# A hybrid encoder layer on one core: first token tiles split straight from PSUM, first block in halves of 256 columns, loads reordered

## The chip, the cores and the metric

The kernel runs on one core of a Trainium2 chip. The metric is the device time of one execution in microseconds (us). Before the change the median of three runs is 2690.09 us (2688.48 to 2690.36). The engines are TensorE (PE in the profile, its weight loads PEld), VectorE (DVE), ScalarE (ACT), GpSimd (POOL) and SyncE (SP), which issues nearly all of the DMA transfers.

## The reference

One layer on 2048 tokens of width 1024 in float32: a mixing step (windowed attention beside a gated linear recurrence), cross-attention into 256 memory tokens, and a SwiGLU feed-forward, each between RMS norms. The change touches only the beginning:

```python
def rms_norm(x, g):
    y = x * lax.rsqrt(jnp.mean(x * x, axis=-1, keepdims=True) + RMS_EPS)
    return y * g

u = rms_norm(h, g_mix_pre[l])      # 2048 x 1024
z = u @ w_in[l]                    # 1024 x 2816
qa, ka, va, qh, fh, ih, gh = jnp.split(z, IN_SPLITS, axis=-1)
```

## The kernel before, in words

**Products.** A float32 product is made of three float32r products: each operand is split into a part `hi` (rounded to float32r) and a rest `lo = x - hi`, and `hi*hi + hi*lo + lo*hi` is summed in PSUM (L915, L916, L917 in `products`). The weights are the stationary operand (tiles `S`), the tokens the moving one (tiles `T`; the first four are called `u`), 128x512 a matmul. Four 2x2 blocks make a group. Groups of kind "s" use a Strassen-like scheme of seven products (`seven`), kind "p" uses plain eight (`eight`). Of the eleven pairs of weight columns in `ORDER`, the first two are kind "p".

**Token tiles of the input projection.** `in_first` makes the operands of the first 1024 tokens. Half s=0 is tokens 0 to 511, half s=1 tokens 512 to 1023; each has four tiles of 128 tokens. q=0 and q=1 are the two halves of the model width. The four operands are called by step: `T[1]` (q=0, s=0), `T[2]` (q=1, s=0), `T[8]` (q=0, s=1), `T[3]` (q=1, s=1). A plain group runs its steps in the order 1, 2, 8, 3, and each step is 24 matmuls: two output blocks of 12.

For each token tile, `norm` does this: ACT squares the tile and sums it (L397, followed by a read of the accumulator), POOL makes the reciprocal root in two small instructions (L95, L97), DVE scales the tile (L399), PE transposes it in eight 128x128 pieces into two PSUM banks (L430), ACT copies each bank to `raw` in SBUF (L432, 128x512), POOL writes `hi` from `raw` (L837), and DVE writes `lo = raw - hi` (L838). `raw` is needed again later: `resident` makes the operands of the steps 5, 6, 7 and 4 from it (L852 to L861).

The weights of a group come in two loads of two DMAs each (`load` in `in_block`; tile `sraw`), and `streamed` splits them into four `S` tiles, on POOL or ACT (L837, L835) and DVE (L838). There are five `S` buffers and three `sraw` buffers. PSUM has six banks of tag `m` (asked for as "g" or "t") and two of tag `s` (asked for as "s" or "h").

**What sets the order.** The code emits instructions in its own order; that is a priority. When the program is built, a list scheduler with a timing model orders the instructions of each engine by that priority and by when it expects their inputs. On the chip each engine takes its instructions strictly in that fixed order, and SP issues its DMAs in order. `phases` is a generator, advanced by `next`: it first asks for the weights of the first group, then for their `S` tiles, then runs all groups.

Before the change `in_first` issues the loads x0, gain, x1, x2, x3, the four weight DMAs of the first group, x4 to x7 (x0 to x7 are the eight token tiles); it emits `norm(0)` (tiles 0 to 3), the first group's `S` tiles, `mix_consts` (small constants of the mixing step), `norm(1)` (tiles 4 to 7), and then the groups.

## Time and profile before

| what | value |
|---|---|
| median of 3 runs | 2690.09 us |
| the profiled execution | 2685.91 us, of which the span from first to last instruction is 2683.9 us |
| mean granted TensorE clock over the span | 0.985 |
| PE busy | 2588.4 us, 96% of the span |
| DVE, ACT, POOL busy | 1691.2, 1236.3, 500.3 us |
| matmuls | 12362 |
| HBM traffic | 168 GB/s over the span |

The page of the profile gives busy time by engine, then the span in 40 slices of 67 us, then the chain of work that ended last, then groups of instructions. "x<-y" is output and inputs; "128x512" is partitions by elements; "idle before" is the time in which the engine waited just ahead of them, with what released it. The views by time (the timeline, the table of windows, the list of waits) answer for a stretch of the span, in us from its start.

### The profile page before, as it was taken

The page shows a single profiled execution, that of the slowest core. Times are in us where ns is not written, and L with a number is a line of the kernel's source. Part 1 is how long each engine was busy: PE and PEld are TensorE (multiplying, and loading weights), DVE is VectorE, ACT ScalarE, POOL GpSimd, SP SyncE. Part 2 cuts the span into 40 slices and gives each one's busy share as a digit, 9 for nine tenths or more (in the row PEclk, how much of TensorE's full clock was granted, in tenths as well). Part 3 has the DMA queues.
Part 4 walks back from the last instruction along what each step waited for, and adds up shares of the span by engine and source line. Part 5 has one row for each costly group of instructions (what it writes and reads, how often), then busy time and mean ns, then how long its engine had stood idle before and what let it go on. Part 6 is the DMA issues. An engine that isn't in the chain of part 4 may idle for free.

```text
span 2683.9 us, 34591 instructions
## 1 busy us (share of the span) xinstructions
PE 2588.4 (96%) x12362; PEld 2162.3 (81%) x12362; DVE 1691.2 (63%) x2643; ACT 1236.3 (46%) x2581; POOL 500.3 (19%) x683
## 2 busy tenths in 40 slices
PE   6989999999988998999989999999999999999998
PEld 5878788887987887888878888888888888888786
DVE  7675578877544657677666555566555556574666
ACT  4453366655423565555554333343333334443443
POOL 5240344321431332223320000000000000000022
PEclk8999999999999999999999999999999999999999
DMA  5434655455877797376793222262222235586988
GB/s 172 138 123 163 185 158 167 127 147 157 241 231 217 200 259 250 103 237 185 215 299 122 76 82 87 87 225 97 95 82 76 85 127 190 192 249 174 290 214 217
DMA packets 394412, 452.25 MB, mean 169 GB/s; under 512 B 19072, under 2 KB 309888, under 8 KB 394240
## 3 DMA queue, kind: packets, MB, share of 16 engines
q1 hardware_dynamic: 383584, 411.25, 47.4%
q0 software_dynamic: 10656, 38.80, 8.2%
q8 instruction: 97, 1.59, 0.3%
q14 instruction: 75, 0.61, 0.1%
HBM read 315.77 MB, written 134.22 MB: 168 GB/s over the span
## 4 chain that ended last, share of the span: by engine, by line
PE 79%; DMA 9%; DVE 3%; POOL 3%; issue 3%; ACT 2%; SPq 1%; POOLq 0%; DVEq 0%; ACTq 0%
PE psm L917 21%; PE psm L915 21%; PE psm L916 21%; PE psg L153 2%; PE psg L151 2%; PE psg L152 2%; DMA row<-in_w_down_dram 1%; PE pss L1101 1%; DMA row<-h_d 1%; DMA row<-in_w_out_dram 1%; DMA row<-in_x_dram 1%; DMA z<-in_w_out_dram 1%; DMA row<-u_d 1%; DVE S L838 0%; DMA h1t_d<-row 0%
## 5 line engine op out<-in xcount | busy, mean ns | idle before, releaser
L915 PE MATMUL psm<-T,S 128*128 128x512 f32 x2726 | 1060.1, 392 | 24.1 <-ACT part L930 12.6
L916 PE MATMUL psm<-T,S 128*128 128x512 f32 x2726 | 1065.1, 391 | 0.5 <-DVE T L838 0.5
L917 PE MATMUL psm<-T,S 128*128 128x512 f32 x2726 | 1056.6, 391 | 1.7 <-DVE S L838 1.7
L915 PEld LDWEIGHTS psm<-T,S 128*128 128x128 f32 x2726 | 514.4, 189 | 134.6 <-ACT part L930 15.1
L917 PEld LDWEIGHTS psm<-T,S 128*128 128x128 f32 x2726 | 513.8, 188 | 109.9 <-DVE S L838 3.5
L916 PEld LDWEIGHTS psm<-T,S 128*128 128x128 f32 x2726 | 514.3, 189 | 106.7 <-DVE T L838 1.2
L838 DVE TENSOR_TENSOR S<-sraw,S 128x512 fp32r<-128x512 f32 (+1 forms) x327 | 228.8, 704 | 253.8 <-ACT S L835 234.4
L835 ACT ACTIVATE S<-sum 128x512 fp32r<-128x512 f32 (+1 forms) x288 | 173.1, 620 | 327.7 <-PE psm L917 232.4
L838 DVE TENSOR_TENSOR S<-sum,S 128x512 fp32r<-128x512 f32 (+1 forms) x340 | 229.6, 685 | 62.7 <-ACT S L835 38.9
L930 ACT ACTIVATE part<-psm 128x512 f32<-128x512 f32 x249 | 147.5, 597 | 224.5 <-PE psm L917 209.3
L1193 POOL DMA_DIRECT2D row<-y_d x28 | 25.9, 926 | 1136.8 <-DVE T L838 971.7
L835 ACT ACTIVATE S<-sraw 128x512 fp32r<-128x512 f32 (+1 forms) x274 | 168.6, 616 | 128.8 <-PE psm L917 114.8
L838 DVE TENSOR_TENSOR T<-row,T 128x1024 fp32r<-128x1024 f32 (+1 forms) x134 | 159.0, 1193 | 75.4 <-ACT T L835 74.3
L835 ACT ACTIVATE T<-row 128x1024 fp32r<-128x1024 f32 (+1 forms) x134 | 137.3, 1032 | 130.2 <-DVE row L852 34.5
L151 PE MATMUL psg<-u,whi 128*128 128x512 f32 x352 | 142.0, 403 | 2.9 <-POOL whi L135 1.7
L153 PE MATMUL psg<-u,wlo 128*128 128x512 f32 x352 | 139.9, 398 | 0.9 <-DVE wlo L136 0.9
L152 PE MATMUL psg<-u,whi 128*128 128x512 f32 x352 | 140.1, 398 | 0.0
L1164 ACT ACTIVATE junk<-row 128x512 f32<-128x512 f32 x160 | 99.9, 626 | 60.8 <-DVE row L1186 17.9
L136 DVE TENSOR_TENSOR wlo<-raw,whi 128x1024 fp32r<-128x1024 f32 x46 | 59.6, 1295 | 38.3 <-POOL whi L135 36.5
L1316 DVE TENSOR_TENSOR row<-psm,part 128x512 f32<-128x512 f32 x60 | 39.9, 688 | 68.8 <-PE psm L917 68.8
L915 PE MATMUL psm<-u,S 128*128 128x512 f32 x172 | 68.8, 403 | 11.5 <-POOL u L837 8.5
L1325 DVE TENSOR_TENSOR part<-psm,part 128x512 f32<-128x512 f32 x60 | 39.7, 688 | 63.4 <-PE psm L917 63.4
(327 smaller groups left out, 3609.0 us busy)
## 6 DMA issues: line engine op xcount, KB each, us to landing
row<-in_w_down_dram SPq DMA_DIRECT2D x53, 512.0 KB, 7.1
sraw<-in_w_gate_dram SPq DMA_DIRECT2D x44, 512.0 KB, 3.6
sraw<-in_w_up_dram SPq DMA_DIRECT2D x44, 512.0 KB, 3.6
row<-u_d SPq DMA_DIRECT2D x44, 512.0 KB, 7.2
hid_d<-row SPq DMA_DIRECT2D x44, 512.0 KB, 2.6
h_d<-row SPq DMA_DIRECT2D x32, 512.0 KB, 5.2
y_d<-row SPq DMA_DIRECT2D x32, 512.0 KB, 3.2
sraw<-hid_d SPq DMA_DIRECT2D x32, 512.0 KB, 5.3
```

The source lines that it names most:

```text
L136: (lo_engine or nc.vector).tensor_tensor(lo, raw, f32(hi), ALU.subtract)
L151: nc.tensor.matmul(ps, ah, bh, start=(i == 0), stop=False)
L152: nc.tensor.matmul(ps, ah, bl, start=False, stop=False)
L153: nc.tensor.matmul(ps, al, bh, start=False, stop=(i == n - 1))
L835: self.nc.scalar.activation(hi, raw, AF.Copy)
L838: self.nc.vector.tensor_tensor(lo, raw, f32(hi), ALU.subtract)
L915: nc.tensor.matmul(ps, s[:, 0, k, :], t[:, 0, k, :], start=st, stop=False, **kw)
L916: nc.tensor.matmul(ps, s[:, 0, k, :], t[:, 1, k, :], start=False, stop=False, **kw)
L917: nc.tensor.matmul(ps, s[:, 1, k, :], t[:, 0, k, :], start=False, stop=sp, **kw)
L930: nc.scalar.activation(t, ps, AF.Copy)
L1164: self.nc.scalar.activation(junk, a, AF.Square, scale=float(D) ** -0.5, accum_out=to)
L1316: nc.vector.tensor_tensor(d, a, c, ALU.add)
```

## The change

For s=0, `raw` is no longer on the way to the operands. `first` has ACT write `hi` straight from the PSUM bank into `T` and DVE write `lo` from the bank and `hi`; POOL has no part in it. The copies to `raw` (`copied`) come later. Tiles 1 and 2 are transposed into banks of tag `m` ("gt"), tiles 0 and 3 into tag `s`. Half s=1 is made as before (`later`), with `mix_consts` behind it. The first group gets a kind "q": its four `S` tiles are made at once, behind the tiles 0 and 1, and its steps 1 and 2 are done for the columns 0 to 255 (token tiles 0 and 1) and then for 256 to 511. The loads become x0, gain, x1, the first two weight DMAs, x2, x3, the other two, x4 to x7.

```diff
-        def norm(s):
-            ...
-            for i in range(4):
-                x = stage[s][:, i, :]
-                self.normed(x, junk[:, i, :])
-                ...
-                    nc.scalar.activation(raw[q, s][:, :, o], ps.rearrange("p (j t) -> p j t", j=4), AF.Copy)
-                    self.split2(raw[q, s][:, :, o], t[:, 0, :, o], t[:, 1, :, o], "P")
+        def copied(s, i, banks):
+            for q in range(2):
+                nc.scalar.activation(raw[q, s][:, :, i * P:(i + 1) * P], banks[q], AF.Copy)
...
+        def first(i, kinds):
+
+            banks = flipped(0, i, kinds)
+            for q in range(2):
+                hi, lo = parts(0, i, q)
+                nc.scalar.activation(hi, banks[q], AF.Copy)
+                nc.vector.tensor_tensor(lo, banks[q], f32(hi), ALU.subtract)
+            return banks
+
+        def later(i):
+            banks = flipped(1, i, "sh")
+            copied(1, i, banks)
+            for q in range(2):
+                self.split2(raw[q, 1][:, :, i * P:(i + 1) * P], *parts(1, i, q), "P")
...
         next(phases)
-        x_loads(1)
-        norm(0)
-        for _ in range(2):
-            next(phases)
+        x_loads(1, range(4))
+        b0 = first(0, "sh")
+        b1 = first(1, "gt")
+        next(phases)
+        b2 = first(2, "gt")
+        copied(0, 0, b0)
+        b3 = first(3, "sh")
+        copied(0, 1, b1)
+        copied(0, 2, b2)
+        copied(0, 3, b3)
+        next(phases)
+        for i in range(4):
+            later(i)
         self.mix_consts()
-        norm(1)
...
         def load(t, j):
+            if between and j:
+                between()
...
-    TAKES = {"s": (1,) * 7, "p": (2, 2, 0, 0)}
+    TAKES = {"s": (1,) * 7, "p": (2, 2, 0, 0), "q": (4, 0, 0, 0)}
...
-    def eight(self, S, T, nk, out, addend):
+    def eight(self, S, T, nk, out, addend, halves=False):
         a11, a21 = S[:2]
         x, y = self.bank("g"), self.bank("t")
-        self.products(x, [(a11, T[1], nk)], True, False)
-        self.products(y, [(a21, T[1], nk)], True, False)
...
+        if halves:
+
+            a12, a22 = S[2:4]
+            del S[:4]
+            for c in range(2):
+                sl = slice(c * 256, (c + 1) * 256)
+                t1, t2 = T[1][:, :, :, sl], T[2][:, :, :, sl]
+                for ps, a, b in ((x, a11, a12), (y, a21, a22)):
+                    self.products(ps[:, sl], [(a, t1, nk), (b, t2, nk)], True, True)
+                if c:
+                    out(0, 0, x, None)
+                    out(1, 0, y, None)
+                yield
```

`flipped` is the norm and the eight transposes of a tile; `parts` gives the `hi` and `lo` slices of an operand for a tile; `between` is `lambda: x_loads(0, (2, 3))` for the first group and nothing for the others.

More of the change, by code (lines that the diff above doesn't have):

```diff
@@ L404, in in_first, with x_loads @@
         stage = []
-        def x_loads(s):
-            t = self.tb.tile([P, 4, D], F32, tag="T", name=f"x0_{s}", bufs=3)
-            for i in range(4):
-                self.load(t[:, i, :], I["x"][(4 * s + i) * P:(4 * s + i + 1) * P, :])
+        def x_loads(s, tiles):
+            if tiles[0] == 0:
+                stage.append(self.tb.tile([P, 4, D], F32, tag="T", name=f"x0_{s}", bufs=3))
+            for i in tiles:
+                self.load(stage[s][:, i, :], I["x"][(4 * s + i) * P:(4 * s + i + 1) * P, :])
                 if s + i == 0:
                     self.g_mix = self.gain(I["g_mix_pre"])
-            stage.append(t)
-        x_loads(0)
+        x_loads(0, (0, 1))
         junk = self.tb.tile([P, 4, D], F32, tag="T", name="x0_j", bufs=3)
@@ L416, in in_first, with flipped, parts @@
         key = {(0, 0): 1, (1, 0): 2, (0, 1): 8, (1, 1): 3}
-        def norm(s):
+        def flipped(s, i, kinds):
+            x = stage[s][:, i, :]
+            self.normed(x, junk[:, i, :])
+            banks = []
+            for q in range(2):
+                ps = self.bank(kinds[q])
+                for j in range(4):
+                    k = 4 * q + j
+                    nc.tensor.transpose(ps[:, j * P:(j + 1) * P], x[:, k * P:(k + 1) * P], self.ident)
+                banks.append(ps.rearrange("p (j t) -> p j t", j=4))
+            return banks
+        def copied(s, i, banks):
+            for q in range(2):
+                nc.scalar.activation(raw[q, s][:, :, i * P:(i + 1) * P], banks[q], AF.Copy)
+        def parts(s, i, q):
+            o = slice(i * P, (i + 1) * P)
+            return T[key[q, s]][:, 0, :, o], T[key[q, s]][:, 1, :, o]
+        def first(i, kinds):
[4 more added lines that the diff above has]
+                nc.vector.tensor_tensor(lo, banks[q], f32(hi), ALU.subtract)
+            return banks
+        def later(i):
+            banks = flipped(1, i, "sh")
+            copied(1, i, banks)
+            for q in range(2):
+                self.split2(raw[q, 1][:, :, i * P:(i + 1) * P], *parts(1, i, q), "P")
+        for s in range(2):
             for q in range(2):
@@ L421, in norm @@
                 raw[q, s] = self.pair_tile().rearrange("p a d -> p (a d)").rearrange("p (k t) -> p k t", k=4)
-            for i in range(4):
-                x = stage[s][:, i, :]
-                self.normed(x, junk[:, i, :])
-                o = slice(i * P, (i + 1) * P)
-                for q in range(2):
-                    ps = self.bank("sh"[q])
-                    for j in range(4):
-                        k = 4 * q + j
-                        nc.tensor.transpose(ps[:, j * P:(j + 1) * P], x[:, k * P:(k + 1) * P], self.ident)
-                    t = T[key[q, s]]
-                    nc.scalar.activation(raw[q, s][:, :, o], ps.rearrange("p (j t) -> p j t", j=4), AF.Copy)
-                    self.split2(raw[q, s][:, :, o], t[:, 0, :, o], t[:, 1, :, o], "P")
         for q in range(2):
@@ L449, in in_first @@
         get = fetch()
-        blocks = [("p" if i < 2 else "s",) + self.in_block(*p, beside[i], get if i > 9 else ())
+        blocks = [("q" if i == 0 else "p" if i < 2 else "s",)
+                  + self.in_block(*p, beside[i], get if i > 9 else (), None if i else lambda: x_loads(0, (2, 3)))
                   for i, p in enumerate(self.ORDER)]
@@ L474, in in_first, with in_block @@
         return u
-    def in_block(self, ca, cb, beside, get):
+    def in_block(self, ca, cb, beside, get, between):
         nc, w = self.nc, self.I["w_in"]
@@ L821, in swa @@
             yield
-    STEPS = {"s": (1, 5, 6, 3, 7, 2, 4), "p": (1, 2, 8, 3)}
-    TAKES = {"s": (1,) * 7, "p": (2, 2, 0, 0)}
+    STEPS = {"s": (1, 5, 6, 3, 7, 2, 4), "p": (1, 2, 8, 3), "q": (1, 2, 8, 3)}
+    TAKES = {"s": (1,) * 7, "p": (2, 2, 0, 0), "q": (4, 0, 0, 0)}
     BLOCK = {1: (0, 0), 8: (0, 1), 2: (1, 0), 3: (1, 1)}
@@ L891, in combine @@
             return t
-        if kind == "p":
+        if kind in "pq":
             for a, e in ((a11, "P"), (a21, "A"), (a12, "P"), (a22, "P")):
@@ L957, in seven @@
             yield
-    def eight(self, S, T, nk, out, addend):
+    def eight(self, S, T, nk, out, addend, halves=False):
         a11, a21 = S[:2]
         x, y = self.bank("g"), self.bank("t")
-        self.products(x, [(a11, T[1], nk)], True, False)
-        self.products(y, [(a21, T[1], nk)], True, False)
-        yield
-        a12, a22 = S[2:4]
-        del S[:4]
-        self.products(x, [(a12, T[2], nk)], False, True)
-        out(0, 0, x, None)
-        self.products(y, [(a22, T[2], nk)], False, True)
-        out(1, 0, y, None)
-        yield
+        if halves:
[10 more added lines that the diff above has]
+                yield
+        else:
+            self.products(x, [(a11, T[1], nk)], True, False)
+            self.products(y, [(a21, T[1], nk)], True, False)
+            yield
+            a12, a22 = S[2:4]
+            del S[:4]
+            self.products(x, [(a12, T[2], nk)], False, True)
+            out(0, 0, x, None)
+            self.products(y, [(a22, T[2], nk)], False, True)
+            out(1, 0, y, None)
+            yield
         x, y = self.bank("g"), self.bank("t")
@@ L1075, in phases @@
                     cur[steps[q][2]] = T[key]
-                run = (self.seven if kind == "s" else self.eight)(ready, cur, nk, out, addend)
+                run = (self.seven(ready, cur, nk, out, addend) if kind == "s" else
+                       self.eight(ready, cur, nk, out, addend, kind == "q"))
                 for q in range(len(self.STEPS[kind])):
```

## The prediction

> **What bounds the kernel now.** I read the page first, then the start of the span, the only stretch the change touches.

> ```profile
> PE 2588.4 (96%) x12362; PEld 2162.3 (81%) x12362; DVE 1691.2 (63%) x2643; ACT 1236.3 (46%) x2581; POOL 500.3 (19%) x683
> ...
> PE   6989999999988998999989999999999999999998
> ...
> PEclk8999999999999999999999999999999999999999
> ```

> PE is the bound: 96% busy, full in nearly every slice. Only the first slice (6 tenths, clock 8 tenths) is poor, so a gain here is PE work that starts earlier. The table of windows (columns: PE, PEld, DVE, ACT, POOL busy, granted clock, DMA share, GB/s) says what PE waits for:

> ```profile
> 10.00:31.00 21.00, 8.76 (x40) 7.14 (x40) 18.61 (x21) 11.92 (x25) 19.71 (x24) 0.71 0.84 244
> 31.00:46.60 15.60, 15.60 (x78) 12.81 (x77) 11.00 (x15) 5.04 (x9) 9.51 (x12) 0.96 0.01 1
> ```
> ```profile
> PE psm L915 <- POOL u L837: 8.5, 1, 8.5
> PE pss L430 <- DVE x L399: 8.0, 1, 8.0
> ...
> POOL u L837 <- ACT pair L432: 5.1, 4, 2.5
> ```

> From 10 to 31 POOL is busy 19.7 of 21 us and DVE 18.6; PE has 8.8. From 31 PE is full. The second fence is the list of waits to 46.6: one wait of 8.5 us, the first product on the last `hi` of s=0, which POOL writes. The timeline of PE shows its end and the next landmark:

> ```profile
> 26.81 1.22 PE L915 MATMUL psm<-u,S 128*128 128x512 f32 x2 [8.53 <-POOL u L837]
> ...
> 30.52 0.78 PE L916 MATMUL psm<-u,S 128*128 128x512 f32 x1
> ...
> 44.67 0.96 PE L915 MATMUL psm<-u,S 128*128 128x512 f32 x3
> ```

> Steady products begin at 30.5. The steps 1 and 2 of group one (48 matmuls), with the transposes of tiles 4 to 7 among them, last until 44.67, where step 8 begins. That mark decides: from there on PE has the same work in both kernels, so what step 8 gains, the kernel gains.

> **The change, part by part.**

> *POOL leaves s=0.* Eight L837 on `u` go, 0.955 us each by mean, 7.6 us of the busy 19.7. POOL keeps its small root pieces and two or three `S`. ACT gets eight `hi` from PSUM in place of eight copies (593 ns a copy, the `hi` of a later line 590), and the copies again afterwards: ACT's sum to step 8 is 8 squares at 1.25, 8 `hi` and 16 copies at 0.59, one `S` at 0.63, about 25 us of the 32 from 4.2 to 36. It is cover, not bound; a square ahead of a `hi` costs at most 1.25.

> *DVE becomes the bound.* It starts, as before, at 6.70 (the gain lands then; x0, gain and x1 are not moved). Its instructions up to the last `lo` that step 8 needs:

> ```profile
> L399 DVE SCALAR_TENSOR_TENSOR x<-x,n_r,g x8: 1273/1627/1632, 6.7 to 32.8; 128x1024 f32<-128x1024 f32 x8
> L838 DVE TENSOR_TENSOR u<-pair,u x16: 674/693/1094, 17.3 to 45.9; 128x512 fp32r<-128x512 f32 x16
> ```
> ```profile
> L501 DVE TENSOR_TENSOR pair<-psm,part x27: 677/691/692, 91.3 to 267.6; 128x512 f32<-128x512 f32 x27
> ```

> (minimum/median/maximum in ns). The first two stretch beside a busy POOL, to 1.63 and 1.09; a subtraction or sum with one input in PSUM (L501) never does, 0.677 to 0.692 in 27. So s=0: 4 scalings at 1.28 (POOL now almost idle), 8 `lo` at 0.69, 4 `S` at 0.68: 5.1 + 5.5 + 2.7 = 13.3. s=1, POOL still in it: 4 scalings at their mean 1.50, 7 `lo` at their mean 0.836: 6.0 + 5.9 = 11.9. Gaps: 1.7 for the first transposes and `hi` (7.98 to about 9.7), and 2.4 as DVE had idle between 10 and 31 (21.0 less 18.6). Step 8 starts at 6.7 + 13.3 + 11.9 + 4.1 = 36.0, against 44.67: **8.7 us earlier**. Ends: all durations at their minimum, one gap: 6.7 + 8 x 1.27 + 15 x 0.68 + 4 x 0.68 + 1.7 = 31.5 (13 earlier); all at their maximum with the gaps: 6.7 + 13.0 + 16.4 + 4.4 + 4.1 = 44.6 (nothing gained).

> [...]

> *Halves.* 48 matmuls of 512 columns become 96 of 256. A row exists, far later, back to back:

> ```profile
> 671.35 0.28 PE L153 MATMUL pss<-mT,wlo 128*128 128x256 f32 x1
> 671.47 0.28 PE L151 MATMUL pss<-mT,whi 128*128 128x256 f32 x1
> ...
> 55.25 0.39 PE L917 MATMUL psm<-u,S 128*128 128x512 f32 x1
> 55.48 0.39 PE L915 MATMUL psm<-u,S 128*128 128x512 f32 x1
> ```

> (The first pair and the second are 616 us apart.) Starts are 0.12 apart against 0.227, so the halves cost 96 x 0.119 - 48 x 0.227 = 0.5 us of PE. That lies under PE's idle time before step 8; without that cover it costs 0.5. What the halves give: tiles 0 and 1 are split by about 15, the `S` by about 17, so 48 matmuls (5.7 us) run to about 23; tile 3 is ready near 22, the other 48 end near 29. Then PE has only transposes (32 more pieces, 0.11 each) until 36.0. That the halves don't wait for the whole operand I take from a pair of rows: POOL wrote a later tile's `hi` at 34.92 while DVE, 34.39 to 35.48, still worked in the same operand on an earlier tile.

> ```profile
> 34.92 1.05 POOL L837 TENSOR_SCALAR u<-pair 128x512 fp32r<-128x512 f32 x1
> 34.39 1.09 DVE L838 TENSOR_TENSOR u<-pair,u 128x512 fp32r<-128x512 f32 x1
> ```

> *The clock.* PE now idles for about 7 us with transposes between, just ahead of step 8. The granted clock was 0.50 from 18.6 to 32.3, with PE idle from 18.3 to 26.8; waits of 3.7 us (before 170.7) and 2.9 us (before 195.5) were each followed by half clock, 0.67 over 172.4 to 177.4 and 0.56 over 196.4 to 200.0: 3.3 and 3.2 us at half speed, that is 1.6 us lost each. I charge 1.6 once. The half clock of before lies ahead of 44.67, so it is in that mark already. [...]

> *Loads.* The weights of the first half (0.5 MB, 1.36 us at the 376 GB/s of 5 to 10) go ahead of x2 and x3: x2, used at 9.24 on landing, comes at 10.6, x3 at 12.0. Their scalings have the turn on DVE at about 14 and 17, so it costs nothing; without that cover 1.4. The queue issues the same DMAs in number; x4 to x7 stay behind the same bytes. The three small loads of `mix_consts` are asked for later; POOL first reads what they give (L509) at 111.8.

> *Downstream.* DVE makes the operands of steps 5, 6 and 7 from 46.6; PE first reads one at 80.64. DVE moves with step 8, so this slack stays. `S` buffers are freed by PE and shift too.

> *Sum.* 8.7 - 1.6 = 7.1 us: the profiled execution would go from 2685.91 to 2678.8, and 2683.0 stands for it against the median 2690.09, which lies 4.2 above that execution.

> **The rivals.**
> 1. *No clock drop, or DVE less stretched*: PE stays busy enough, or s=1 runs at minimum durations: 8.7 to 13 us, 2677.1 to 2681.4. For: POOL has little else; against: both engines still meet in s=1. 0.20.
> 2. *DVE stretched or badly ordered*: s=1 at 1.63 and 1.09 and a few us of gaps, as its build-time order may put PE's transposes behind a blocked product (as at 26.81, where two L915 stood ahead of transposes). Step 8 between 39 and 44.6; less the clock, 0 to 4 us: 2686 to 2690. 0.26.
> 3. *The halves don't do what they say*: a half waits for the whole operand. Then 96 matmuls run from 22 (11.4 us) with the transposes (3.5): 36.9, no idle, no drop: 44.67 - 36.9 = 7.8, 2682.3. The rows at 34.92 speak against. 0.05.
> 4. *Slower.* The schedule of the later groups is built anew from a shifted start. In the recurrence's groups PE waits for ACT, which stands in a fixed order behind table loads and DVE scans: waits of 1.8, 3.7 and 2.9 us at 145, 167 and 193. One more of 3.7 with its 1.6 of clock costs 5.3. From two on the gain of 7.1 is gone (+3.5, 2693.6); three give 2698.9. For: such waits are there, and nothing reserves against them; against: the groups' own code and inputs are unchanged, and a pure shift leaves them be. 0.16.

> **The numbers.** A measurement here can tell about 0.2%, 5.4 us. The forecast (step 8 at 35 to 38, one drop) has 0.33, of which 0.30 lies beyond 5.4 us. Faster: 0.30 + 0.20 + 0.05 = 0.55. Same: 0.03 + 0.26 = 0.29. Slower: 0.16. The range runs from 2676.5, below the minimum durations, to 2695.5, past two new stalls; some 0.04 is left out below and 0.16 above. The forecast with rivals 1 and 3 alone would be 2677 to 2685.

> **What will show it.** Right: L838 on `u` from PSUM at 0.69; first 128x256 product near 17; second half from about 22; step 8's first 128x512 product near 36 with DVE, not POOL, named ahead of it; granted clock 0.5 there for some 3 us; POOL idle more than half of 10 to 31. Wrong: step 8 near 44 (DVE stretched), no 256-column product before tile 3's `lo` (rival 3), or the same start with longer PE waits at 140 to 200 (rival 4).

## The result, and the profile after

Five runs of the changed kernel gave a median of 2676.90 us (2674.36 to 2682.49), five of the kernel before, on the same chip, 2688.48 (2683.44 to 2690.36): a ratio of 0.9961, 95% interval 0.9945 to 0.9978. In a later set of runs, nine of the changed kernel, the same pair gave 0.9975 (0.9965 to 0.9984). By the two ratios that is 10.5 and 6.7 us less, by the medians 11.6 and 6.5. The profiled execution took 2676.90 us with a span of 2675.0; its span is 8.9 us shorter than that of before. Lines of the code moved by 35: L950 to L952 are the products, L872 and L873 POOL's `hi` and DVE's `lo`, L428 the transposes, L434 the copies, L445 and L446 the new `hi` and `lo` from PSUM.

The page of the changed kernel, busy time by engine and the rows of PE and of its clock by slice:

```profile
PE 2587.2 (97%) x12410; PEld 2163.8 (81%) x12410; DVE 1688.1 (63%) x2643; ACT 1239.6 (46%) x2589; POOL 489.3 (18%) x675
...
PE   7999999999988998999989999999999999999998
...
PEclk9999999999999999999999999999999999999999
```

The first slice (0 to 67 us) went from 6 to 7 tenths and its clock from 8 to 9. The third (134 to 201 us) went from 8 to 9, and that is one that the change doesn't touch. The table of windows of the changed kernel (PE, PEld, DVE, ACT, POOL busy, granted clock, DMA share, GB/s):

```profile
10.00:31.00 21.00, 16.10 (x104) 15.21 (x105) 17.09 (x24) 14.99 (x31) 11.96 (x18) 1.00 0.82 251
31.00:46.60 15.60, 14.04 (x87) 11.73 (x86) 13.29 (x14) 9.77 (x17) 7.96 (x10) 1.00 0.12 35
```

From 10 to 31 PE does 16.1 us of work instead of 8.8, POOL 12.0 instead of 19.7. But behind 31 PE is no longer full: 1.6 us are idle. Its timeline in the changed kernel shows the first product in halves, the wait inside the second half (two of its products, on `hi` alone, ran from 25.45 on), step 8 and the first product on a `T` made from `raw`:

```profile
16.96 0.78 PE L950 MATMUL psm<-u,S 128*128 128x256 f32 x2
...
27.38 0.38 PE L951 MATMUL psm<-u,S 128*128 128x256 f32 x1 [1.53 <-DVE u L446]
...
39.90 0.96 PE L950 MATMUL psm<-u,S 128*128 128x512 f32 x3 [0.91 <-POOL u L872]
...
75.39 0.39 PE L950 MATMUL psm<-T,S 128*128 128x512 f32 x1
```

Step 8 starts 4.77 us earlier (44.67 before), the first `T` product 5.25 (80.64). The same products later on are 5.2 us earlier up to 150, about 4 at 175 to 189, 7.3 at 249 (256.25 before), 9.0 at 388 and 8.9 at the end; in between the lead is 7.5 at 700 and 10.0 at 1000. So in these two executions some 5 us were won at the start, and almost 4 more between 190 and 390, where the code is the same. There PE's waits changed. In the kernel before, and then in the changed one:

```profile
195.56 0.50 PE L915 MATMUL psm<-u,S 128*128 128x512 f32 x1 [2.94 <-ACT S L835]
```
```profile
189.70 0.50 PE L950 MATMUL psm<-u,S 128*128 128x512 f32 x1 [1.27 <-ACT S L870]
```

The wait is 1.67 us shorter, and behind it the clock of before was halved for 3.41 us (from 196.14), that of the changed kernel was not: about 1.7 us of work. A wait of 1.27 us for the output tile `z` at 293 in before has no counterpart. Two questions were left: which part of the change wins the start, and what it has to do with a wait at 190.

### The profile page after: what moved, and what is told of

Same layout as the page of the kernel before. It is cut to its first block, busy times and chain, and to the rows that moved or that the text cites. A ratio compares the mean times of both kernels' runs of the same rounds, so it can differ in the third digit from the quotient of the medians.

```text
span 2675.0 us, 34685 instructions
## 1 busy us (share of the span) xinstructions
PE 2587.2 (97%) x12410; PEld 2163.8 (81%) x12410; DVE 1688.1 (63%) x2643; ACT 1239.6 (46%) x2589; POOL 489.3 (18%) x675
## 3 DMA queue, kind: packets, MB, share of 16 engines
q8 instruction: 97, 1.59, 0.2%
## 4 chain that ended last, share of the span: by engine, by line
PE 79%; DMA 10%; DVE 4%; POOL 3%; issue 2%; ACT 2%; SPq 1%; POOLq 0%; DVEq 0%; ACTq 0%
PE psm L952 21%; PE psm L950 21%; PE psm L951 21%; PE psg L153 3%; PE psg L152 3%; PE psg L151 3%; DMA row<-in_w_down_dram 1%; PE pss L1151 1%; DMA row<-in_w_out_dram 1%; DMA row<-h_d 1%; DMA row<-in_x_dram 1%; DMA row<-qk_d 1%; DMA z<-in_w_out_dram 1%; DMA raw<-in_wo_x_dram 1%; DMA row<-u_d 1%
## 5 line engine op out<-in xcount | busy, mean ns | idle before, releaser
L950 PE MATMUL psm<-T,S 128*128 128x512 f32 x2726 | 1060.7, 393 | 23.2 <-ACT part L965 12.4
L952 PE MATMUL psm<-T,S 128*128 128x512 f32 x2726 | 1057.1, 391 | 2.5 <-DVE S L873 2.5
L950 PEld LDWEIGHTS psm<-T,S 128*128 128x128 f32 x2726 | 514.9, 189 | 133.2 <-ACT part L965 14.5
L952 PEld LDWEIGHTS psm<-T,S 128*128 128x128 f32 x2726 | 514.5, 189 | 111.0 <-DVE S L873 4.2
L873 DVE TENSOR_TENSOR S<-sraw,S 128x512 fp32r<-128x512 f32 (+1 forms) x327 | 227.6, 701 | 253.1 <-ACT S L870 233.8
L873 DVE TENSOR_TENSOR S<-sum,S 128x512 fp32r<-128x512 f32 (+1 forms) x340 | 229.1, 684 | 62.0 <-ACT S L870 39.1
L873 DVE TENSOR_TENSOR T<-row,T 128x1024 fp32r<-128x1024 f32 (+1 forms) x134 | 158.4, 1190 | 76.0 <-ACT T L870 75.1
L151 PE MATMUL psg<-u,whi 128*128 128x512 f32 x352 | 141.8, 403 | 1.6 <-POOL whi L135 1.6
L153 PE MATMUL psg<-u,wlo 128*128 128x512 f32 x352 | 140.2, 398 | 0.9 <-DVE wlo L136 0.9
L1366 DVE TENSOR_TENSOR row<-psm,part 128x512 f32<-128x512 f32 x60 | 39.9, 688 | 68.5 <-PE psm L952 68.5
L136 DVE TENSOR_TENSOR wlo<-raw,whi 128x1024 fp32r<-128x1024 f32 x46 | 60.4, 1312 | 35.9 <-POOL whi L135 35.8
L135 POOL TENSOR_SCALAR whi<-raw 128x1024 fp32r<-128x1024 f32 x46 | 53.6, 1166 | 135.1 <-PE psg L152 34.7
```

What stands on the lines that cost most here:

```text
L135: nc.gpsimd.tensor_scalar(hi, raw, 1.0, 1.0, ALU.mult, ALU.mult)
L136: (lo_engine or nc.vector).tensor_tensor(lo, raw, f32(hi), ALU.subtract)
L151: nc.tensor.matmul(ps, ah, bh, start=(i == 0), stop=False)
L153: nc.tensor.matmul(ps, al, bh, start=False, stop=(i == n - 1))
L873: self.nc.vector.tensor_tensor(lo, raw, f32(hi), ALU.subtract)
L950: nc.tensor.matmul(ps, s[:, 0, k, :], t[:, 0, k, :], start=st, stop=False, **kw)
```

## Experiments

Times are given as ratio to the kernel before on the same chip, since its median lay between 2682 and 2689 us in the four sets of runs.

**One part at a time.** `split_only` has the new split, but the old loads and products of 512 columns; `halves_only` is the kernel before with the first group as kind "q"; `no_halves` and `no_loads` are the changed kernel less one part:

```diff
-                       self.eight(ready, cur, nk, out, addend, kind == "q"))
+                       self.eight(ready, cur, nk, out, addend))
```
```diff
-        x_loads(0, (0, 1))
+        x_loads(0, range(4))
...
-                  + self.in_block(*p, beside[i], get if i > 9 else (), None if i else lambda: x_loads(0, (2, 3)))
+                  + self.in_block(*p, beside[i], get if i > 9 else (), None)
```

The first edit is `no_halves`, the second `no_loads`, both together `split_only`. `halves_only` takes `eight` as in the change, with this in before:

```diff
-        blocks = [("p" if i < 2 else "s",) + self.in_block(*p, beside[i], get if i > 9 else ())
+        blocks = [("q" if i == 0 else "p" if i < 2 else "s",) + self.in_block(*p, beside[i], get if i > 9 else ())
```

> The direct split of s=0 alone (with its banks and late copies): loads in the old order, step 1 and 2 in 512 columns. Theory A (the direct split takes POOL out and sets the gain): step 8 starts between 38 and 41, 4 to 6 us before the 44.67 of the kernel before, and the time is 5 to 10 us shorter than before. Rival (the halves and the loads carry it): step 8 starts at 43 or later and under 3 us are gained.

> The kernel before, with steps 1 and 2 of the first group in halves of 256 columns and its four S made at once; split over raw and POOL, loads in the old order. Theory A: the operands come no earlier, so step 8 starts at 44 to 45 and the time is within 3 us of before. Rival (the halves carry the gain): first 256-column product by 23, step 8 by 41, 5 us or more gained.

> The changed kernel with steps 1 and 2 in 512 columns again. Theory A: the halves hide under the wait for step 8; step 8 within 1.5 us of the 39.90 of the changed kernel, time within 3 us of it. Rival (halves let PE start 10 us sooner and that counts): step 8 at 42 or later, and 2 us or more of the gain lost.

> The changed kernel with the loads in the old order (x2 and x3 ahead of the weights). Theory A: tile 2 comes 1.4 us sooner, the S later, DVE has the same work: step 8 within 1.5 us of 39.90. Rival (the early weights are needed for the first products): first products 2 us or more later than 16.96 and step 8 at 41 or later.

| kernel | ratio (95%) | step 8 | first T | wait near 190 to 196 | wait near 293 |
|---|---|---|---|---|---|
| before | 1 | 44.67 | 80.64 | 2.94 | 1.27 |
| split_only | 0.9992 (0.9982 to 1.0001) | 42.23 | 77.76 | 2.59 | 1.03 |
| no_halves | 1.0000 (0.9990 to 1.0010) | 43.65 | 79.15 | 2.57 | 2.46 |
| halves_only | 0.9976 (0.9966 to 0.9985) | 41.68 | 77.18 | 1.25 | under 0.4 |
| no_loads | 0.9967 (0.9954 to 0.9980) | 39.06 | 76.66 | 1.24 | none |
| changed | 0.9961 and 0.9975 | 39.90 | 75.39 | 1.27 | none |

The theory behind the forecast, that the split straight from PSUM makes the gain and the halves are hidden, fell: without the halves nothing is left that can be told from no change, and the halves alone give 0.24%. The whole changed kernel, run again on the same chip as these four, gives 0.25% (`after_again`, 0.9975): the split and the loads add nothing to the halves that the times can tell. The steps at the start fit neither theory neatly: step 8 of split_only, 42.23, is later than theory A had it and earlier than the rival, and the 41.68 of halves_only lies between the two as well. In the start the halves are worth 3.8 us (first `T` 79.15 against 75.39): without them PE's first product comes at 22.32 and steady ones from 24.96, when tile 3's `lo` is made, against 16.96. From 24.96 to step 8 at 43.65 PE is then busy but for 0.5 us, so there PE itself sets that mark. Part of the 3.8 is the clock: the products of no_halves are 0.43 apart up to 30.68, while the changed kernel does its slow ones ahead of 20.5. These are single traces; `before_mid4` below, which is the kernel before but for four small products, has its first `T` at 79.38 against 80.64, with half clock to 29.7 instead of 32.3. And the later waits go by the halves too: 2.6 to 2.9 us in the three kernels without, 1.24 to 1.27 in the three with. Behind the first stage `halves_only` differs from before in the place of one load on SP and one instruction of ACT. What it does have is 48 matmuls more.

**Where 48 matmuls reach the wait at 195.** That wait ends a chain: ACT's `S` stands in its fixed order behind the gates of the recurrence, these for DVE, and DVE stands in its order at a sum of weights. Its row in no_halves and in the changed kernel:

```profile
186.09 0.69 DVE L925 TENSOR_TENSOR sum<-sraw,sraw 128x512 f32<-128x512 f32 x1 [3.83 <-DMA sraw<-in_w_in_dram]
```
```profile
180.51 0.69 DVE L925 TENSOR_TENSOR sum<-sraw,sraw 128x512 f32<-128x512 f32 x1 [2.53 <-DMA sraw<-in_w_in_dram]
```

The list of DMA queues, from the issue of that load (two DMAs of 256 KB) to the sum, says what differs; no_halves (180.8 to 186.1) first, then the changed kernel (176.5 to 180.6). The lines of figures are GB/s in 40 equal parts of the stretch; then queue, kind: packets, MB, share of 16 engines:

```profile
GB/s 62 0 0 0 0 0 0 0 39 58 73 112 220 305 336 348 352 333 352 321 332 456 247 104 23 0 0 0 0 12 8 8 12 8 12 12 0 0 0 0
...
q1 hardware_dynamic: 1064, 0.53, 34.7%
q8 instruction: 1, 0.02, 1.1%
```
```profile
GB/s 0 0 0 0 0 0 0 0 0 0 15 65 55 45 120 85 155 245 305 345 350 335 345 345 345 350 350 340 355 255 165 100 45 5 0 0 0 0 0 0
...
q1 hardware_dynamic: 1059, 0.52, 44.0%
```

In no_halves a packet of queue q8, "instruction", of 0.02 MB falls into the load. Most of the load is through at some 184.1; then a trickle of 8 to 12 GB/s goes on from 184.6 to 185.6. I read it as the share of the one engine that the other transfer held for about 1 us, an estimate: the 1.1% of 16 engines over 5.3 us are 0.93 us of one engine, and no view shows an engine alone. DVE's sum starts at 186.09, behind the last of it. Over the whole span q8 has 97 packets and 1.59 MB, 16 KB each, at 127 matmuls a packet (12362 / 97). I take them for PE's own instructions, which the profile doesn't say: 12362 matmuls and as many weight loads are 255 a packet. Then, by estimate, 48 matmuls put ahead of them move every packet 48 x 0.227 = 10.9 us earlier in the work.

**Useless products to move the packets.** If this is so, matmuls that nobody reads must do what the halves do. `no_halves_pad48` puts 48 at the very start of no_halves, `after_pad80` 80 at the start of the changed kernel (80 + 48 = 128, about one packet by that count):

```diff
+        idr = self.cst.tile([P, P], F32R, name="idr")
+        nc.gpsimd.tensor_scalar(idr, self.ident, 1.0, 1.0, ALU.mult, ALU.mult)
+        idle = self.bank("h")
+        for i in range(48):
+            nc.tensor.matmul(idle[:, 0:P], idr, idr, start=True, stop=True, skip_group_check=True)
```

`before_mid4`, `before_mid32` and `before_mid48` have 4, 32 and 48 in the kernel before, in PE's idle time ahead of its first product:

```diff
         norm(0)
+        idle = self.bank("h")
+        for i in range(32):
+            nc.tensor.matmul(idle[:, 0:P], T[1][:, 0, 0, 0:P], T[1][:, 0, 0, 0:P], start=True, stop=True, skip_group_check=True)
```

> This is the kernel with 512-column products (no halves) and 48 more matmuls at the very start: 128x128 products of the identity with itself that nobody reads. They bring PE's count of matmuls to that of the changed kernel; behind the first stage the order of every engine is that of no_halves. Theory F (instruction fetch): PE's own instructions come in 16 KB pieces through a DMA queue, about every 128 matmuls; in the kernels without halves one piece falls at 183 to 185 us, on the same DMA engines as the weight load that DVE waits for, and another at 281; 48 matmuls more put the pieces at about 168 to 172 and 200, as in the kernels with halves. F expects: the weights at the DVE sum near 180 land about 3.0 us after their last issue instead of 4.3, the PE wait near 195 is 1.2 to 1.3 us instead of 2.57, no half clock follows it, the wait near 293 is under 0.5 us, and from the first T product to 340 us it takes 3 to 4 us less than no_halves (median 2684 to 2686 if the start stays that of no_halves, first T near 79). Theory S (the products in halves help by what they make start earlier, so a shift of the start or the order): the waits of 2.6 and 1.0 to 2.5 and the half clock stay, time as no_halves (2688.6) plus what the start loses, 0 to 2 us.

> The changed kernel with 80 such identity products at the very start. With the 48 of the halves they are 128, one whole piece of instructions by the distance of the pieces seen (30 us of products at 0.227), so the pieces fall again where they fall without halves. Theory F expects: a piece at about 180 (with the start's shift), the DVE sum's weights land over 4 us after their last issue, the PE wait near 190 is 2.4 to 3 us and half clock follows it, and the wait of over 1 us at some 288 is back: 3 to 5 us lost behind the first T product, against the changed kernel. Theory S: those waits stay at 1.25 and below 0.5, and only what the 80 products delay at the start is lost, 0 to 4 us by the first T product.

> The kernel before with 4 useless products (128x128, of the first token tile's hi part with itself) in PE's idle time ahead of the first product. The order of every engine is otherwise that of before. Control: theory F (instruction fetch) has the piece of PE's instructions at about 183, 0.9 us earlier than before, still inside the landing of the weights that DVE waits for (issued at 180.7): landing over 4 us after the last issue, wait near 195 of 2.3 to 3 us with half clock behind it, ratio 0.999 to 1.001. Theory S (only an earlier start or another order changes the later waits): the same.

> The same with 32 such products. The order of ACT and POOL is that of before; on SP one load and on DVE one instruction change places with a neighbour. They fit into PE's idle 8.5 us at 0.22 us each (7 us), so the first T product stays at 80 to 81.5. Theory F: the pieces come 7.3 us earlier, at about 176.5 and 273.5, so the weights at 186 land 3.0 us after their last issue, the wait near 195 falls to 1.2 to 1.9 us and no half clock follows it, the wait near 293 is under 0.5 us: 2 to 4 us less than before although PE does more, ratio 0.9985 to 0.9993, unless the moved pieces meet another load. Theory S: waits and time as before, ratio 0.9995 to 1.001.

> The same with 48 such products, which makes PE's count that of the changed kernel, while nothing of its split, its halves or its loads is there; they need some 10.5 us and the idle time is 8.5 to 11, so the first T product stays at 80 to 82.5. Theory F: the pieces come 10.9 us earlier, at about 173 and 270, weights landing 3.0 us after their last issue, wait near 195 of 1.2 to 1.9 us without half clock behind it, wait near 293 under 0.5 us: behind the first T product 3 to 4 us less than before, ratio 0.9985 to 0.9995 with what the start loses. Theory S: waits as before, ratio 1.000 to 1.001.

> The changed kernel once more, beside the three below on one chip. Both theories: 0.4% under the kernel before (ratio 0.994 to 0.998); first T product near 75.4, wait near 190 of 1.2 to 1.3 us without half clock behind it, none over 0.5 us at 284 to 294.

"Landing" is from the end of the second issue of that load to the sum; times of the packet are counted from the end of PE's wait some 25 us earlier (170.7 in before). The load is issued at +9.9 to 11.2:

| kernel | packet at | landing | wait near 195 | first T | ratio (95%) |
|---|---|---|---|---|---|
| before | +13.0 | 4.71 | 2.94 | 80.64 | 1 |
| split_only | +13.2 | 4.36 | 2.59 | 77.76 | as above |
| no_halves | +12.8 | 4.34 | 2.57 | 79.15 | as above |
| after_pad80 | +12.8 | 4.07 | 2.30 | 86.98 | 1.0036 (1.0024 to 1.0048) |
| before_mid4 | +11.5 | 4.27 | 2.49 | 79.38 | 0.9998 (0.9988 to 1.0008) |
| no_halves_pad48 | not there | 3.02 | 1.25 | 80.21 | 1.0005 (0.9994 to 1.0015) |
| before_mid32 | not there | 3.00 | 1.23 | 81.66 | 0.9993 (0.9985 to 1.0002) |
| before_mid48 | not there | 3.35 | 1.57 | 83.48 | 0.9995 (0.9986 to 1.0005) |
| after_again | not there | 3.36 | 1.60 | 75.51 | 0.9975 (0.9965 to 0.9984) |
| halves_only, no_loads, changed | not there | 3.00 to 3.04 | 1.24 to 1.27 | 75.39 to 77.18 | as above |

The landing follows the packet in all twelve traces, in both directions: 4.07 to 4.71 with it, 3.00 to 3.36 without; four useless products leave it, 32 take it away, 80 bring it back. The wait follows: 2.30 to 2.94 against 1.23 to 1.60. Another order of the instructions is no rival for this: behind the first stage no_halves_pad48 has the order of no_halves on every engine, and the load on SP that changed its place in before_mid32, before_mid48 and halves_only did so in split_only as well, which has the packet. The sum and the wait of before_mid4 and then of before_mid32:

```profile
184.93 0.69 DVE L893 TENSOR_TENSOR sum<-sraw,sraw 128x512 f32<-128x512 f32 x1 [3.75 <-DMA sraw<-in_w_in_dram]
...
194.10 0.50 PE L918 MATMUL psm<-u,S 128*128 128x512 f32 x1 [2.49 <-ACT S L838]
```
```profile
188.37 0.69 DVE L893 TENSOR_TENSOR sum<-sraw,sraw 128x512 f32<-128x512 f32 x1 [2.48 <-DMA sraw<-in_w_in_dram]
...
197.55 0.50 PE L918 MATMUL psm<-u,S 128*128 128x512 f32 x1 [1.23 <-ACT S L838]
```

That shows what makes this wait longer or shorter. What it is worth in time is less firm. before_mid32 and before_mid48 reach the first `T` product 1.0 and 2.8 us late, and by their ratios they are 1.9 and 1.3 us below before (by the medians 1.4 and 2.5): 3 to 4 us won behind it, as expected. But both intervals hold 1, so the gain itself is not shown. Nor is the count alone the gain of the halves: with 48 useless products and a start 2.8 us later before_mid48 stays at 0.9995 (0.9986 to 1.0005), with 48 more and a start 3.5 us earlier halves_only comes to 0.9976 (0.9966 to 0.9985). no_halves_pad48 shows none either (1.0005) and has a longer wait at a new place: 5.00 us at 274.9, where POOL, with its weights earlier, works beside DVE, whose `lo` of those weights (L136) takes 2.06 us there and 1.21 in the changed kernel (the two pairs of instructions ahead of it take 3.21 and 2.54 against 2.36 and 2.13). That was not expected. after_pad80 has one of 4.99 at 283.0, and none near 288, where one was expected back; it ends 9.7 us above before, of which 6.3 are lost at the start (86.98 against 80.64; it is 11.6 behind the changed kernel there, where 0 to 4 were expected); the returned packet and that wait are in the rest.

The wait near 293 is not settled. In the three kernels where it is over 1 us and has a packet near (281 to 282: before, split_only, no_halves) the loads of `kr` land 4.6 us after their issue in before against 3.4 in the changed kernel; but before_mid48 has a wait of 1.18 at 292.0 with no packet near.

**Half clock by windows.** Behind the wait comes a second price. Windows of no_halves, then of the changed kernel (PE busy, granted clock, DMA share, GB/s):

```profile
191.25:194.60 3.35, 1.46 (x9) 1.00 0.00 0
194.70:198.05 3.35, 2.78 (x6) 0.50 0.00 0
198.10:201.45 3.35, 3.35 (x9) 0.50 0.65 223
```
```profile
160.50:163.85 3.35, 1.32 (x10) 1.00 0.17 70
163.95:167.30 3.35, 1.45 (x4) 0.50 0.21 82
167.35:170.75 3.40, 3.40 (x10) 0.50 0.54 154
170.85:174.20 3.35, 3.35 (x17) 1.00 0.70 215
187.75:191.20 3.45, 1.98 (x10) 1.00 0.00 0
191.25:194.60 3.35, 3.35 (x16) 1.00 0.41 157
```

**Step 8 earlier.** Two tries to get below 39.9: other banks for tiles 4 and 6, and besides that half s=1 split from PSUM as well:

```diff
-            banks = flipped(1, i, "sh")
+            banks = flipped(1, i, ("gt", "sh", "gt", "sh")[i])
```

and in later_direct

```diff
-            copied(1, i, banks)
             for q in range(2):
-                self.split2(raw[q, 1][:, :, i * P:(i + 1) * P], *parts(1, i, q), "P")
+                hi, lo = parts(1, i, q)
+                nc.scalar.activation(hi, banks[q], AF.Copy)
+                nc.vector.tensor_tensor(lo, banks[q], f32(hi), ALU.subtract)
+            copied(1, i, banks)
```

> The changed kernel with only the banks of tiles 4 and 6 changed from tag s to tag m. Theory B (tile 4's transposes at 30.35 and with them all of s=1 wait for the banks of tag s, freed at 28.5): the transposes of tile 4 come 3 us or more earlier and step 8 starts at 37 to 38.5. Theory D (POOL's and DVE's turns set it): tile 4 earlier, but step 8 at 39 to 40 and the time within 1 us of the changed kernel.

> The changed kernel with the tiles of s=1 split straight from PSUM as well (ACT hi, DVE lo) and their copies to raw behind it; tiles 4 and 6 transposed into banks of tag m. Theory D (step 8 is held at 39.9 by POOL and DVE taking turns on s=1 and by the banks of tag s): POOL leaves, step 8 starts at 35 to 37 and the time falls by 2 to 4 us against the changed kernel, if the first T product follows. Theory E (the end of the first stage is set by DVE alone, whose order and stretch stay): step 8 at 39 to 40 and no change beyond 1 us. The copies come later here, so a first T product that doesn't move (75.4) would say that ACT has become the bound. PE's count of matmuls is unchanged, so theory F puts its instruction pieces where the changed kernel has them.

`later_banks` came to 1.0012 (1.0002 to 1.0021), `later_direct` to 1.0013 (1.0002 to 1.0023): both are no faster than before (the changed kernel was not run in that set). The operands of step 8 are indeed ready earlier (DVE's last `lo` at 36.98 in later_banks), but the order made at build time now has the transposes of tiles 3, 4 and 5 ahead of all products, and PE reaches its first at 27.86 instead of 16.96. Step 8 starts at 41.99 and 41.91, later than any of the theories had it, and the first `T` product comes at 77.38 and 77.30. Tile 4's transposes did come earlier (21.46 in later_banks, 30.35 in the changed kernel), as theory B had it; what held step 8 at 39.9 was not tested apart, since the order moved with the banks. And the order of the later groups changed with it. PE's timeline in later_banks:

```profile
150.57 0.79 PE L950 MATMUL psm<-T,S 128*128 128x512 f32 x1 [7.86 <-ACT part L965]
```

The changed kernel has waits of 1.86 and 4.03 there (141.6 and 165.8). Near 196 both have waits of 2.96 and 2.91, although no packet meets their weights (landing 3.03 and 3.00): in another order another instruction is late. This is the mechanism of the forecast's fourth rival, met in a kernel that is two banks away.

## Why the prediction was right, and where it was not

The gain was forecast at 7.1 us and came out at 9.0 in the profiled execution, 6.7 and 10.5 by the two ratios. The median of the changed kernel, 2676.90, is 6.1 us below the forecast of 2683.0 and only 0.4 above the lower end of the range. The mechanism was right in part: POOL left s=0, and step 8 came earlier. That the number holds is luck: the start gave 4.8 us in place of 8.7, and the runs give most of that to the halves, which were counted at nothing; the charge of 1.6 for the clock was not paid; and some 4 us came from a place that was counted at nothing.

*POOL leaves, DVE becomes the bound: right in the sum of the work, wrong in the gaps and in what is named ahead of step 8.* From 6.65 to 39.90 DVE is busy for 25.4 us; the forecast had 13.3 + 11.9 = 25.2. The step that failed is the term of the gaps: 4.1 forecast, 33.25 - 25.36 = 7.9 measured, and that is the whole difference between 36.0 and 39.9. That the work agrees is luck too: DVE also does 3.0 us that the list lacks (small constants of the mixing step, 1.0, a scaling of a later tile, 1.28, and a fifth `S`, 0.68), and instructions without a gap between them overlap in the trace by some 0.08 us each (25.45 + 1.27 against 26.65 in the rows below), 2.0 in all. And the first product of step 8 waits for POOL's `hi` (the row of 39.90 above), where DVE was to be named. DVE in the changed kernel:

```profile
25.45 1.27 DVE L399 SCALAR_TENSOR_TENSOR x<-x,n_r,g 128x1024 f32<-128x1024 f32 x1
26.65 1.28 DVE L446 TENSOR_TENSOR u<-pss,u 128x512 fp32r<-128x512 f32 x2
32.32 1.69 DVE L873 TENSOR_TENSOR u<-pair,u 128x512 fp32r<-128x512 f32 x2 [4.40 <-POOL u L872]
```

The gap of 4.40 us comes from the fixed orders, as the second rival had it. DVE does all four scalings of s=1 (20.00 to 26.7) ahead of tile 3's `lo`, although its `hi` was there at 24.6. So PE's second half, two products of `hi` aside, waits until 27.38, tile 3's two banks are free at 28.5, and tile 4, scaled since 21.3, is transposed only at 30.35, behind half of those products. POOL is idle for 7.07 us before 31.67, then POOL and DVE work on s=1 side by side, about 1 us a piece, to the end. That rival priced it at a start of 39 to 44.6, and 39.90 lies there; its time, 2686 to 2690, did not come.

*`lo` from PSUM at 0.69: right.* Eight times 0.673 to 0.683 us, while the `lo` of s=1 beside POOL took 0.988 by mean (0.836 forecast). POOL was idle for 9.0 of the 21 us from 10 to 31, not for more than half.

*Halves: right in their price, wrong as hidden.* They start at 16.96 (17 forecast) before tile 2's `lo` is made, so they don't wait for the whole operand. The second half runs from 27.38, not from about 22. Their 0.5 us of PE don't show. But they were said to end long before DVE lets step 8 go, and to give nothing; they give 3.8 us of the start, since without them PE itself, not DVE, sets step 8 (43.65); and with PE's count of instructions they shift its packets (at +12.8 in no_halves, none there in the changed kernel).

*The clock charge: not paid.* The record shows no half clock from 0 to 163 (on the first products see the last section), and the products of step 8 are 0.23 apart from 40.70 on. PE was to idle for 7 us before step 8; with the second half ending at 33.74 and the transposes of tiles 5 to 7 behind it, the longest wait is 0.91. It was paid in no_loads, where the wait ahead of step 8 is longer:

```profile
39.06 0.96 PE L950 MATMUL psm<-u,S 128*128 128x512 f32 x3 [1.79 <-POOL u L872]
```

There the clock is halved from 40.57 to 43.98, and the first `T` product comes 1.27 us after that of the changed kernel although step 8 started 0.84 ahead. So the loss that was charged does occur, behind a wait of 1.79 us. And PE was not idle throughout every window that half clock followed: in before it was busy for 1.72 of the 3.41 us from 762.8, and the clock was 0.50 from 766.2 to 769.6.

*Loads: right that they cost nothing* (no_loads, 0.9967). *Downstream slack: right for the first `T` product*, which doesn't wait in any of the kernels. *"From there on PE has the same work, so what step 8 gains, the kernel gains": wrong.* PE has the same work, but the packets of its instructions, as I read the experiments, meet the weights on the DMA engines (landing 4.07 to 4.71 us with the packet, 3.00 to 3.36 without), and their places moved by 48 matmuls; besides, the wait of 2.57 us in no_halves was followed by two windows of half clock, that of 1.27 in the changed kernel by none.

## What to carry to other kernels

Count on fixed orders before durations: an estimate by an engine's sum of work leaves the idle time out, and here the idle time that the build-time order leaves was 7.9 us against 25.4 of work. If a change alters the number of instructions of an engine early in a long program, look at the list of DMA queues for "instruction" packets beside the waits that changed later on, before looking for a cause in the code. And compare several traces of one kernel before a difference of 1 to 2 us in a wait is called a gain: here two traces of the changed kernel had 4.03 and 2.38 us for one wait, 1.27 and 1.60 for another.

## What the hardware showed that was not expected

With one 16 KB packet of queue q8, "instruction", beside it, a load of 512 KB landed 0.9 to 1.4 us later: issued at about +10, in 4.27 to 4.71 us against 3.35; issued at +10.7 to 11.2, in 4.07 to 4.36 against 3.00 to 3.04.

The granted clock that the profile shows did not agree with the products ahead of its first change. In the changed kernel it reads 1.00 from the start to 163.9, but the products of 256 columns are 0.21 apart at first and 0.12 only from 20.6 on:

```profile
20.25 0.41 PE L950 MATMUL psm<-u,S 128*128 128x256 f32 x1
20.46 0.34 PE L951 MATMUL psm<-u,S 128*128 128x256 f32 x1
20.64 0.28 PE L952 MATMUL psm<-u,S 128*128 128x256 f32 x1
```

The same shows in no_halves: its products of 512 columns are 0.43 apart up to 30.68 and 0.23 from 30.98 on, at a granted clock of 1.00. So in both the first products came at a little over half the rate of later ones, at a clock shown as full. The 9 of the first slice in the row of the clock, against the 8 of before, is then in part, I take it, a matter of when the first change was recorded: at 18.6 in before, at 163.9 in the changed kernel.
